# State-space outputs: states stored chunk-contiguous, all Toeplitz products first, then state products alternating over row halves and two PSUM banks

## The chip, the cores and the metric

The kernel runs on one core of a Trainium2 chip. The metric is the time of one execution on the device, in microseconds (us). The core has the matrix engine TensorE (PE; its weight loads are listed as PEld), VectorE (DVE), ScalarE (ACT), GpSimd (POOL) and SyncE (SP), which here mostly issues DMA transfers. Each engine works through a queue of its own, in order. PE multiplies a stationary operand, which is loaded first, with a moving one, and adds the result up in one of eight PSUM banks.

## What is computed

One layer of a decoder: normalisation, one input projection for two parallel parts, a sparse attention of eight heads and a state-space layer, then an output projection and a gated feed-forward network (FFN). The change concerns the state-space layer. For each of 32 groups of 16 channels it has 64 complex diagonal states:

```python
bu_re = jnp.einsum('blgi,gpi->blgp', uf, bb_re)
bu_im = jnp.einsum('blgi,gpi->blgp', uf, bb_im)
...
_, _, h_re, h_im = lax.associative_scan(complex_affine_combine, (ar, ai, bu_re, bu_im), axis=1)
y = (jnp.einsum('blgp,gip->blgi', h_re, prm['ssm_c_re'].astype(f32))
     - jnp.einsum('blgp,gip->blgi', h_im, prm['ssm_c_im'].astype(f32))
     + prm['ssm_d'].astype(f32) * uf)
```

The prompt has 1024 tokens, beside it there are 8 samples of 4 tokens. `y` goes through a gated linear unit (GLU) and, with the attention's output, into the output projection.

## The kernel before

The state-space layer is cut into 128 chunks of 8 tokens. A chunk's output is the sum of two parts: a Toeplitz product of the chunk's own inputs, and a product of the state before the chunk with C times powers of the eigenvalues. Groups go in pairs (two groups g of 64 states fill the 128 partitions), 16 pairs, four quarters Q of four pairs.

- `ssm_input` writes each chunk's contribution V (PE, line 1508) into the tile `H` (ssm_H; ACT, line 1511). `H` is laid out [128 states, 129 chunks, real/imaginary, 16 pairs].
- `ssm_scan` turns them into states: 128 steps of four DVE instructions of 32 elements each (lines 1526 to 1529), spread over the second phase, which is about the samples' attention and the first tiles of the prompt's.
- `ssm_powers` makes `Ct`, C times the powers, on POOL.
- `ssm_kernel(Q)`, letter K in the plan, makes the Toeplitz matrices: products `Kp` for g = 0 and 1 (PE, line 1576), four copies each, alternately on ACT and DVE (line 1579), an addition of the direct term `dd` on DVE (line 1584), and eight DMA loads on SP into `W[Q % 2]` (ssm_W, line 1586).
- `ssm_output(Q)`, letter Y, makes the outputs: for each g one PSUM bank `Y` with four pairs j side by side. For each j stand one Toeplitz product (line 1599, stationary operand the inputs ssm_UT, 128 rows) and two states' products (line 1601, stationary operand `self.H[P[g], 0:128, i, jj]`, 64 rows, one of real and imaginary part i). All are fp32 and each is two instructions on PE. ACT copies the bank out (line 1603). Then come the samples' outputs `Ys` in the same way (lines 1610, 1613, 1616), and DMAs to y_d and ys_d.

These pieces stand between the products of the prompt's attention (`phase_attend`, the third phase). Eight tiles of 128 prompt tokens are treated in the order 4, 0, 6, 1, 7, 2, 5, 3, each in four units (branch br, half hf): scores `as` for four heads (PE, lines 1195, 1196, 1199), maximum `asm` (DVE, line 1211), exponential `ap` (ACT, line 1212), then transposes (line 1269) and values `aso` (line 1273); `acs` (line 1248) and `aco` belong to the compressed branch. `PLAN` names what goes between the units, so for tile 0: nothing, nothing, `K0 K1 Y0`, `K2 Y1`; for tile 6: `K3 Y2`, `Y3 S`, `W G7`, `T4 G8 T5`. S are the last states, W the GLU's weights, G its tiles, T the second part of the modulation, P the output projection's weights.

The program's order is a wish: the framework's scheduler fixes each engine's own order at build time, by its own simulation, within the limits that buffers set. PSUM in this phase has a tag "s" of two tiles of two banks each, "t" with two banks, "o" and "f" with one each. Scores take "s". Within the planned pieces `ps_t` gives the one bank of "f" (`tags, self.tags = self.tags, "ff"`), so `Kp`, `Y` and `Ys` of the kernel before all go through that one bank, one after another.

Of the kernel before, what the change touches and what calls it, by code (L numbers as in the profile page):

```python
# [20 lines left out]
D = 1024  # L21
NT = 8          # tiles of 128 prompt tokens
NK = 8          # tiles of 128 input features
# [5 lines left out]
def shape_constants():  # L29
    """Constants that depend on shapes and positions alone, packed as [128, n] columns."""  # L30
# [27 lines left out]
    # sample rows are (batch in the half, token, group, head in the group)  # L58
# [31 lines left out]
class Kernel:  # L90
# [35 lines left out]
    def psum(self, name, **tags):  # L126
        self.pp = self.open(name, space=PS)
        self.pbufs = tags
        self.tags = "to"
        for t in tags:      # the banks go to the tags in this order  # L130
            self.pp.tile([128, 512 * (2 if t == "s" else 1)], F32, tag=t, name=f"{name}_{t}", bufs=tags[t])
# [23 lines left out]
    def load_constants(self, ea):  # L155
# [26 lines left out]
        nc.vector.tensor_scalar(self.gain_q, self.gain_q, 0.125, None, op0=ALU.mult)     # with the scores' scale  # L182
        # vectors over features, turned to feature-major: b_ada 48, norm_mix_g 8, norm_ffn_g 8, attn_out_g 4, ssm_out_g 4
# [12 lines left out]
    # ---- 1/sqrt(x * a + b), elementwise, on a small tile: a guess from the exponent, scaled by c, and three of Newton's  # L196
    # steps without their factor of -1/2, so that the scale turns c into -2 c^3, three times, and ends at one ----
    def rsqrt(self, x, a, b, name, eng=None, tag="", pool=None, bufs=3):
# [5 lines left out]
        # the guess: the bits of (magic - half of the bits) with c in its exponent and sign  # L204
        V.tensor_scalar(y.bitcast(I32), s.bitcast(I32), -0.5, float(0x5F3759DF) + math.log2(-c) * 2 ** 23 - 2 ** 31, op0=ALU.mult, op1=ALU.add)
        for _ in range(3):
            V.tensor_tensor(t, y, y, op=ALU.mult)
            V.tensor_tensor(t, t, s, op=ALU.mult)
            if eng:     # only the vector engine does both at once
# [22 lines left out]
    def ada_features(self, nb, ev, out):  # L232
        """out [128 feature, 4, 9] for the four 128-feature blocks, with the bias."""
# [8 lines left out]
    def ada_rows(self, nb, ev, pool, dst):  # L242
        """the nine rows, with the bias, to DRAM."""
# [34 lines left out]
    def phase_project(self):  # L278
        self.psum("psa", s=2, t=3, o=1)
        self.adaT = self.cst.tile([128, 4, 8, 9], F32, name="adaT")   # shift1, (1 + scale1) gain, and the FFN's  # L280
# [92 lines left out]
    def prep_c(self, pa):  # L373
        """silu of the nine conditions, feature-major; they come as rows (row, k-tile) of 128."""
# [26 lines left out]
    def gather(self, out, cache, b, j):  # L401
        """four positions of each of the 128 16-position chunks of a batch's paged rows: [128, 1024]."""
# [4 lines left out]
    def split(self, raw, hi, lo):  # L407
        """raw = hi + lo, each of twelve bits."""
        self.nc.scalar.copy(hi, raw)  # L409
        self.nc.vector.tensor_tensor(lo, raw, hi.bitcast(F32), op=ALU.subtract)  # L410

    def compress_weights(self, pa, pb):
# [4 lines left out]
        for i, s in enumerate("kv"):  # L417
# [16 lines left out]
            # the encodings' part of the hidden layer: products summed over the positions, then over the partitions  # L434
# [13 lines left out]
    def compress(self, b, cp):  # L448
        """the compressed keys and values of a paged batch (the ninth is the prompt), four positions of each chunk at a
        time; the products of one part follow the turning of the next, and the output's product comes later still."""  # L450
# [23 lines left out]
    def c_turn(self, b, j, cp):  # L474
        """four positions turned and split, two positions times 64 on the partitions: [(hi, lo)] of keys and values."""
# [27 lines left out]
    def c_product(self, b, j, X, cp):  # L503
        """their part of the hidden layer, for the blocks that begin and the blocks that end with the chunk."""
# [51 lines left out]
    def gelu2(self, out, x, t):  # L556
        """twice the tanh form of gelu: x (1 + tanh(sqrt(2 / pi) (x + 0.044715 x^3))); t is scratch."""
# [7 lines left out]
    def sigmoid2(self, out, z):  # L565
        """twice the sigmoid: 1 + tanh(z / 2)."""
# [31 lines left out]
    def sample_modulate(self, xn, out, iscale, ishift, p):  # L598
        """xn [32, 1024] normalised rows to feature-major modulated out [128, 8, 32]."""
# [10 lines left out]
    def sample_qkv(self, ea, sa):  # L610
# [20 lines left out]
        # gates, as rows (b, t, g, r) of three  # L631
# [7 lines left out]
        # queries, block-diagonal over the two groups  # L639
# [22 lines left out]
    def sample_attend(self, half, sb):  # L662
        """a half of the sample batches; rows (batch, token, group, head). The keys come in runs of 512 cached ones
        (the last run of a branch has the new ones behind it), each with its own maximum; the runs are weighed at the end. It goes in seven steps,
        the second half's between the products of the prompt's attention."""
# [7 lines left out]
        # compressed branch  # L673
# [15 lines left out]
        # importance of the 30 blocks that are not forced, the ranks, the mask of those not among the best 13  # L689
# [27 lines left out]
        # the new keys' scores, of both other branches  # L717
# [42 lines left out]
        # weights of the runs: exp(their maximum - the largest) gate / sum; M holds the maxima negated  # L760
# [1128 lines left out]
```

## Time and profile before

| | us |
|---|---|
| median of 3 runs | 1857.84 |
| lowest and highest | 1857.72 to 1870.4 |
| span of the profiled execution | 1867.2 |
| PE busy in it | 1779.7 (95%) |

The profile is of one execution by itself. Its page gives the span, 1867.2 us from the first to the last instruction, and no other time for that execution; it is 9.4 us above the median of the runs. Times of single instructions and of gaps come from this execution. "PEclk" is the granted clock of PE as a share of its full speed. The views give, beside the page, groups of instructions by line, single rows in order of time, sums over windows of time, and the chain of waits that ended last.

### The profile page before, as it was taken

The numbers are of one execution on the slowest core, as the hardware profiler recorded it, in microseconds if no ns is written. First come the engines' busy times: TensorE is split into PE (matmuls) and PEld (weight loads), VectorE is DVE, ScalarE is ACT, GpSimd is POOL, SyncE is SP. The second block draws the span as 40 slices with busy tenths as digits, with TensorE's granted clock in tenths as the row PEclk, the third lists the DMA queues.
The fourth block names the chain that finished last, engine by engine and source line by source line (L and its number), as shares of the span: only waits on it lengthen the run. The fifth ranks groups of instructions, "written<-read, shape, count | busy, mean of one in ns | idle before, by whom it ended". The sixth has DMA issues, their size and how long they took to land.

```text
span 1867.2 us, 29377 instructions
## 1 busy us (share of the span) xinstructions
PE 1779.7 (95%) x11546; PEld 1476.4 (79%) x11546; DVE 953.9 (51%) x2330; ACT 632.4 (34%) x1263; POOL 423.4 (23%) x817
## 2 busy tenths in 40 slices
PE   6898999899898999999989989999999999999997
PEld 3788998777655676565658889999999999999996
DVE  4867657667978433655755452332332332332346
ACT  4422146455555342565643341211211211211210
POOL 2334645232025310333112210100100100100140
PEclk9999999999899886999999999999999999999999
DMA  8333244544141111544225331201201201201113
GB/s 290 103 83 111 73 141 125 214 149 157 58 142 66 27 37 31 174 158 155 87 91 178 102 113 46 68 23 46 68 23 46 68 23 46 68 23 46 51 46 139
DMA packets 132700, 172.44 MB, mean 92 GB/s; under 512 B 17177, under 2 KB 92313, under 8 KB 132305
## 3 DMA queue, kind: packets, MB, share of 16 engines
q1 hardware_dynamic: 123024, 136.62, 23.0%
q0 software_dynamic: 9408, 33.89, 5.7%
q8 instruction: 91, 1.49, 0.3%
q14 instruction: 49, 0.39, 0.1%
q10 hardware_dynamic: 128, 0.04, 0.0%
HBM read 143.88 MB, written 25.46 MB: 91 GB/s over the span
## 4 chain that ended last, share of the span: by engine, by line
PE 83%; DVE 8%; DMA 4%; ACT 3%; issue 2%; POOL 0%; SPq 0%; another core or an unknown queue 0%; DVEq 0%; ACTq 0%; POOLq 0%
PE gu L1793 18%; PE dn L1836 13%; PE g L1793 5%; PE u L1793 4%; PE cp L516 4%; PE aso L1273 4%; PE Y L1601 2%; PE as L1195 2%; PE ss L823 1%; PE as L1196 1%; PE q0p L927 1%; PE ct L494 1%; PE q1p L927 1%; PE u1p L927 1%; PE kv0p L927 1%
## 5 line engine op out<-in xcount | busy, mean ns | idle before, releaser
L1793 PE MATMUL gu<-h2h,wh 128*128 128x352 f32 x704 | 227.9, 324 | 5.0 <-ACT h2h L860 5.0
L1793 PE MATMUL gu<-h2h,wl 128*128 128x352 f32 x704 | 227.4, 323 | 0.0
L1793 PE MATMUL gu<-h2l,wh 128*128 128x352 f32 x704 | 226.9, 322 | 0.0
L1842 DVE TENSOR_TENSOR acc<-acc,dn 128x512 f32<-128x512 f32 x144 | 98.8, 686 | 229.6 <-PE dn L1836 229.6
L1801 POOL TENSOR_TENSOR al<-fa,ah 128x352 fp32r<-128x352 f32 (+1 forms) x66 | 69.5, 1053 | 415.1 <-ACT ah L1800 408.8
L1796 ACT ACTIVATE fa<-gu 128x352 f32<-128x352 f32 x44 | 20.4, 465 | 412.5 <-PE gu L1793 412.5
L1836 PE MATMUL dn<-dh,ah 128*128 128x512 f32 x352 | 140.4, 399 | 5.2 <-DVE fin L1845 4.6
L1793 PEld LDWEIGHTS gu<-h2h,wh 128*128 128x128 f32 x704 | 132.6, 188 | 7.9 <-ACT h2h L860 5.3
L1836 PE MATMUL dn<-dl,ah 128*128 128x512 f32 x352 | 138.7, 394 | 0.0
L1836 PE MATMUL dn<-dh,al 128*128 128x512 f32 x352 | 138.3, 393 | 0.0
L1793 PEld LDWEIGHTS gu<-h2l,wh 128*128 128x128 f32 x704 | 133.0, 189 | 3.8
L1793 PEld LDWEIGHTS gu<-h2h,wl 128*128 128x128 f32 x704 | 132.9, 189 | 3.0
L409 ACT CAST wh<-wr 128x1024 fp32r<-128x1024 f32 x44 | 46.0, 1048 | 154.2 <-PE g L1793 77.0
L1799 DVE TENSOR_TENSOR fa<-fa,gu 128x352 f32<-128x352 f32 x44 | 22.9, 521 | 143.8 <-ACT fa L1796 143.8
L1195 PE MATMUL as<-kst,aqA 128*128 128x320 f32 (+4 forms) x192 | 79.7, 420 | 7.0 <-ACT ap L1212 2.9
L1836 PEld LDWEIGHTS dn<-dh,ah 128*128 128x128 f32 x352 | 66.1, 188 | 24.3 <-ACT wh L409 7.5
L410 DVE TENSOR_TENSOR wl<-wr,wh 128x1024 fp32r<-128x1024 f32 x44 | 58.8, 1338 | 49.8 <-ACT wh L409 49.8
L1836 PEld LDWEIGHTS dn<-dl,ah 128*128 128x128 f32 x352 | 66.1, 188 | 15.6
L1836 PEld LDWEIGHTS dn<-dh,al 128*128 128x128 f32 x352 | 66.3, 188 | 8.1
L1211 DVE TENSOR_REDUCE asm<-as 128x1 f32<-128x640 f32 (+3 forms) x64 | 58.7, 921 | 26.1 <-PE as L1199 25.5
L1196 PE MATMUL as<-kst,aqB 128*128 128x320 f32 (+4 forms) x192 | 67.4, 355 | 4.4 <-ACT aqB L1158 4.2
L1212 ACT ACTIVATE ap<-as,asm 128x640 f32<-128x640 f32 (+3 forms) x64 | 55.8, 874 | 27.4 <-DVE asm L1211 17.4
(2135 smaller groups left out, 4735.6 us busy)
## 6 DMA issues: line engine op xcount, KB each, us to landing
wada<-in_w_ada SPq DMA_DIRECT2D x24, 1024.0 KB
wr<-in_w_ffn_gate SPq DMA_DIRECT2D x22, 512.0 KB
wr<-in_w_ffn_up SPq DMA_DIRECT2D x22, 512.0 KB
wd<-in_w_ffn_down SPq DMA_DIRECT2D x22, 512.0 KB
bx<-in_x_prompt SPq DMA_DIRECT2D x8, 512.0 KB
s_raw<-in_cache_kv_win SPq DMA_DIRECT2D x8, 512.0 KB
wor<-in_w_out SPq DMA_DIRECT2D x16, 256.0 KB
ex<-x_d SPq DMA_DIRECT2D x8, 512.0 KB
```

What stands on the lines that cost most here:

```text
L410: self.nc.vector.tensor_tensor(lo, raw, hi.bitcast(F32), op=ALU.subtract)
L516: nc.tensor.matmul(P[:, 256 * ab:256 * ab + 256], w[:, 8 * ab + 2 * j + i, :], x[:, i, :], start=j == 0 and i == 0 and n == 0 and ab == 0, ...
L927: nc.tensor.matmul(p[:, t, :n], h[:, k, tok], ww[:, k % 4, :n], start=m == 0, stop=m == 23)
L1195: nc.tensor.matmul(Sv, qA[:, h, :], kk, start=True, stop=False)
L1196: nc.tensor.matmul(Sv, qB[:, h, :], kk, start=False, stop=not mt)
L1211: nc.vector.tensor_reduce(mx[:, :1], Sv, axis=ax, op=ALU.max, negate=True)
L1212: nc.scalar.activation(Pv, Sv, AF.Exp, bias=mx[:, :1], accum_out=l[:, h:h + 1])
L1273: nc.tensor.matmul(O[64 * g:64 * g + 64, 256 * hf:256 * hf + 256], V[:n, 64 * g:64 * g + 64], pT[:, 256 * g:256 * g + 256], start=first, s ...
L1793: nc.tensor.matmul(gu[i], w[:, k, :], h[:, k, 352 * n:352 * n + 352], start=m == 0, stop=m == 23)
L1801: nc.gpsimd.tensor_tensor(al[:, cols], a[:, :w], ah[:, cols].bitcast(F32), op=ALU.subtract)
L1836: nc.tensor.matmul(p, a[:, sl], w[:, c], start=m == 0, stop=m == 5)
L1842: nc.vector.tensor_tensor(o, o, p, op=ALU.add)
```

## The change

`H` is stored as [128 states, real/imaginary, 16 pairs, 129 chunks], so the 128 chunks of one pair lie next to each other: the stationary operand of a states' product is contiguous, while a step of the scan and the last state are read and written at a step of 129 elements, 516 bytes. `Y` becomes one tile of the tag "s" with a bank for each g. Its eight Toeplitz products come first; then the sixteen states' products in the order pair j, part i, group g, so that rows 0 to 63 with the first bank and rows 64 to 127 with the second alternate. ACT copies the bank of g = 0 out and DVE that of g = 1. `Ys` is changed likewise; its four copies take both groups at once. The count of matmuls stays. (The changed file also has no comments any more, which moves line numbers by a few.)

```diff
     def ssm_input(self, Q, sp, Bt):
...
-            nc.scalar.copy(self.H[:, 1:, :, jj], pv[:, :, :128].rearrange("p r c -> p c r"))
+            nc.scalar.copy(self.H[:, :, jj, 1:], pv[:, :, :128])
             nc.vector.tensor_copy(self.Hs[:, :, :, jj], pv[:, :, 128:])
...
     def ssm_scan(self, ss):
...
-            h = H[:, c]
-            hx = bass.AP(tensor=h.tensor, offset=h.offset + 16, ap=[h.ap[0], [-16, 2], [1, 16]])
+            h = H[:, :, :, c]
+            hx = bass.AP(tensor=h.tensor, offset=h.offset + 16 * 129, ap=[h.ap[0], [-16 * 129, 2], [129, 16]])
             V.tensor_tensor(t[0], LA[:, 0], h, op=ALU.mult)
             V.tensor_tensor(t[1], LA[:, 1], hx, op=ALU.mult)
             V.tensor_tensor(t[0], t[0], t[1], op=ALU.add)
-            V.tensor_tensor(H[:, c + 1], H[:, c + 1], t[0], op=ALU.add)
+            V.tensor_tensor(H[:, :, :, c + 1], H[:, :, :, c + 1], t[0], op=ALU.add)
...
-            nc.tensor.transpose(p[:16, :128], H[:, 128, i], self.ident)
+            nc.tensor.transpose(p[:16, :128], H[:, i, :, 128], self.ident)
...
     def ssm_output(self, Q):
...
+        Y = self.ps_s(f"Y{Q}")
         for g in G:
-            Y = self.ps_t(f"Y{Q}{g}")
             for j in range(4):
-                jj = 4 * Q + j
-                y = Y[:, 128 * j:128 * j + 128]
-                nc.tensor.matmul(y, self.UT[:, 2 * jj + g, :128], Wf[:, 2 * j + g], start=True, stop=False)
-                for i in range(2):
-                    nc.tensor.matmul(y, self.H[P[g], 0:128, i, jj], Ct[i][P[g], j, 1:9, :].rearrange("p t o -> p (t o)"),
-                                     start=False, stop=i == 1)
-            nc.scalar.copy(o[:, :, :, g, :].rearrange("c t j o -> c j t o"), Y.rearrange("c (j t o) -> c j t o", j=4, t=8))
+                nc.tensor.matmul(Y[:, g, 128 * j:128 * j + 128], self.UT[:, 8 * Q + 2 * j + g, :128], Wf[:, 2 * j + g],
+                                 start=j == 0, stop=False, skip_group_check=True)
+        for j in range(4):
+            for i in range(2):
+                for g in G:
+                    nc.tensor.matmul(Y[:, g, 128 * j:128 * j + 128], self.H[P[g], i, 4 * Q + j, 0:128],
+                                     Ct[i][P[g], j, 1:9, :].rearrange("p t o -> p (t o)"), start=False, stop=i == 1, skip_group_check=True)
+        for g in G:
+            (nc.vector.tensor_copy if g else nc.scalar.copy)(o[:, :, :, g, :].rearrange("c t j o -> c t j o"),
+                                                             Y[:, g].rearrange("c (j t o) -> c j t o", j=4, t=8))
...
+        Ys = self.ps_s(f"Ys{Q}")
         for g in G:
-            Ys = self.ps_t(f"Ys{Q}{g}")
             for j in range(4):
-                nc.tensor.matmul(Ys[32 * j:32 * j + 8, :64], self.UT[:, 8 * Q + 2 * j + g, 128:136], Wf[:, 2 * j + g, 64:], start=True, stop=False)
-            for i in range(2):
-                for j in range(4):
-                    nc.tensor.matmul(Ys[32 * j:32 * j + 8, :64], self.h0[P[g], i, :, 4 * Q + j],
-                                     Ct[i][P[g], j, 1:5, :].rearrange("p t o -> p (t o)"), start=False, stop=i == 1)
+                nc.tensor.matmul(Ys[32 * j:32 * j + 8, g, :64], self.UT[:, 8 * Q + 2 * j + g, 128:136], Wf[:, 2 * j + g, 64:],
+                                 start=True, stop=False, skip_group_check=True)
+        for i in range(2):
             for j in range(4):
-                nc.vector.tensor_copy(o[:, :, j, g], Ys[32 * j:32 * j + 8, :64].rearrange("c (t o) -> c t o", t=4))
+                for g in G:
+                    nc.tensor.matmul(Ys[32 * j:32 * j + 8, g, :64], self.h0[P[g], i, :, 4 * Q + j],
+                                     Ct[i][P[g], j, 1:5, :].rearrange("p t o -> p (t o)"), start=False, stop=i == 1, skip_group_check=True)
+        for j in range(4):
+            (nc.scalar.copy if j % 2 else nc.vector.tensor_copy)(
+                o[:, :, j].rearrange("c t g o -> c g t o"), Ys[32 * j:32 * j + 8, :, :64].rearrange("c g (t o) -> c g t o", t=4))
...
     def ssm_start(self, ss, si):
...
-        self.H = self.small(ss, [128, 129, 2, 16], "ssm_H")
+        self.H = self.small(ss, [128, 2, 16, 129], "ssm_H")
         self.Hs = self.small(ss, [128, 2, 8, 16], "ssm_Hs")
-        nc.vector.memset(self.H[:, 0], 0.0)
+        nc.vector.memset(self.H[:, :, :, 0], 0.0)
```

With the new tiles the scheduler also builds another order. PE's queue before, at the first piece of Y (quarter 0, g = 0): numbers behind names count buffers, Ct_7715 is the real part's and Ct_7716 the imaginary part's; a row is one matmul as the program writes it.

```order
L1269 MATMUL as601pt_8589<-ident,ap_8339 128x128
L1599 MATMUL Y_8067<-ssm_W_7711,ssm_UT_7709 128x128
L1601 MATMUL Y_8067<-Ct_7715,ssm_H 128x128
L1601 MATMUL Y_8067<-Ct_7716,ssm_H 128x128
L1599 MATMUL Y_8067<-ssm_W_7711,ssm_UT_7709 128x128
L1601 MATMUL Y_8067<-Ct_7715,ssm_H 128x128
L1601 MATMUL Y_8067<-Ct_7716,ssm_H 128x128
```

The two kinds of product change places after every one or two, and scores and values of the attention follow the piece. PE's queue after, from the last values of tile 6's first unit to Y1 (Kp_8041 is K1 for g = 1, Kp_8136 is K2 for g = 0, Y_8175 and ssm_W_7712 are quarter 1's):

```order
L1273 MATMUL aso_8335<-as606pT_8390,vst 64x256 x2
L1598 MATMUL Y_8067<-ssm_W_7711,ssm_UT_7709 128x128 x8
L1603 MATMUL Y_8067<-Ct_7715,ssm_H 128x128 x2
L1603 MATMUL Y_8067<-Ct_7716,ssm_H 128x128 x2
L1576 MATMUL Kp_8041<-Ct_7725,ssm_par 16x128 x4
L1576 MATMUL Kp_8041<-Ct_7726,ssm_par 16x128 x4
...
L1614 MATMUL Ys_8096<-ssm_W_7711,ssm_UT_7709 8x64 x8
L1619 MATMUL Ys_8096<-Ct_7715,ssm_par 8x64 x8
L1619 MATMUL Ys_8096<-Ct_7716,ssm_par 8x64 x8
L1576 MATMUL Kp_8136<-Ct_7735,ssm_par 16x128 x4
L1576 MATMUL Kp_8136<-Ct_7736,ssm_par 16x128 x4
L1598 MATMUL Y_8175<-ssm_W_7712,ssm_UT_7709 128x128 x8
```

The rows left out are the other twelve states' products of Y0. Between Y0 and Y1 no scores or values stand any more, and the second half of K1 is inside Y0. The scores of tile 6's second unit stood among K0's products before, one head of them here:

```order
L1195 MATMUL as_8337<-kst,aqA_7916 128x512
L1196 MATMUL as_8337<-kst,aqB_7917 128x512
L1195 MATMUL as_8337<-kst,aqA_7916 128x384
L1196 MATMUL as_8337<-kst,aqB_7917 128x384
L1199 LDWEIGHTS identb
L1199 MATMUL as_8337<-mk,identb 128x128
L1269 MATMUL as601pt_8358<-ident,ap_7940 128x128
```

After, all four heads of that unit stand behind Ys1 and the first Kp of K3:

```order
L1619 MATMUL Ys_8204<-Ct_7726,ssm_par 8x64 x8
L1576 MATMUL Kp_8400<-Ct_7745,ssm_par 16x128 x4
L1576 MATMUL Kp_8400<-Ct_7746,ssm_par 16x128 x4
L1195 MATMUL as_8295<-kst,aqA_7916 128x512
L1196 MATMUL as_8295<-kst,aqB_7917 128x512
L1195 MATMUL as_8295<-kst,aqA_7916 128x384
```

Later pieces follow: the GLU's tiles, the modulation's blocks and the output projection's weights stand earlier in the queues than before. The order of the scan's instructions on DVE is the same.

## Rows read from the trace of the kernel before

**Rows 1.** The page: span, busy time of PE, weight loads and the other engines.

```profile
span 1867.2 us, 29377 instructions
...
PE 1779.7 (95%) x11546; PEld 1476.4 (79%) x11546; DVE 953.9 (51%) x2330; ACT 632.4 (34%) x1263; POOL 423.4 (23%) x817
```

**Rows 2.** Windows (us, length, busy time by engine) at low and full clock.

```profile
core 0: us, PE busy (x) PEld busy (x) DVE busy (x) ACT busy (x) POOL busy (x), PEclk, DMA share, GB/s
...
619.00:626.00 7.00, 7.00 (x27) 4.97 (x29) 2.28 (x5) 1.47 (x3) 4.01 (x10) 0.51 0.11 19
...
639.50:660.00 20.50, 20.50 (x173) 13.99 (x171) 9.23 (x20) 10.34 (x24) 0.00 (x0) 1.00 0.10 16
...
704.30:724.80 20.50, 20.42 (x117) 13.74 (x117) 4.01 (x12) 2.93 (x5) 0.00 (x0) 0.50 0.09 27
```

**Rows 3.** Windows of the seven low stretches, tile Y alone: their sum.

```profile
sum 58.70, PE 22.73 PEld 17.42 ACT 4.16; mean PE 3.25 PEld 2.49 ACT 0.59
```

**Rows 4.** Windows of the eight pieces of Y, instructions of Y alone.

```profile
615.21:621.56 6.35, 6.35 (x24) 5.07 (x24) 0.00 (x0) 0.80 0.28 45
...
713.33:720.75 7.42, 7.42 (x24) 5.63 (x24) 0.00 (x0) 0.50 0.01 2
...
sum 51.43, PE 51.43 PEld 41.07 ACT 0.00; mean PE 6.43 PEld 5.13 ACT 0.00
```

**Rows 5.** Tile Y: weight loads, xcount: ns min/median/max, first and last start.

```profile
L1601 PEld LDWEIGHTS Y<-Ct,ssm_H x128: 287/310/313, 615.5 to 729.8; 64*128 64x128 f32 x128
L1599 PEld LDWEIGHTS Y<-ssm_W,ssm_UT x64: 186/189/338, 615.1 to 728.6; 128*128 128x128 f32 x64
```

**Rows 6.** Chain of waits, 570 to 905 us: start us, us, what.

```profile
611.46 1.73 PE acs L1248 x16
...
617.08 1.07 PE Y L1601 x4
...
618.57 1.17 PE Y L1601 x4
```

**Rows 7.** Timeline of PE, 338 us: start us, us, engine, line, operation, xcount.

```profile
338.23 1.15 PE L1508 MATMUL V<-ssm_UT,BTs 128*64 128x136 f32 x16
```

**Rows 8.** Timeline of PE, 624 to 642 us.

```profile
624.84 1.12 PE L1273 MATMUL aso<-as600pT,vst 128*64 128x256 f32 x4
...
625.75 0.65 PE L1273 MATMUL aso<-as601pT,vst 128*64 128x256 f32 x4
...
641.24 0.41 PE L1613 MATMUL Ys<-Ct,ssm_par 64*8 64x64 f32 x16
```

**Rows 9.** Timeline, 608 to 621 us, all engines.

```profile
608.07 0.58 SPq L1582 DMA_DIRECT2D dd<-in_ssm_d  x1
...
609.93 0.58 DVE L1583 TENSOR_TENSOR dd<-dd,ident 16x128 f32<-16x128 f32 x1 [0.42 <-DMA dd<-in_ssm_d]
...
610.51 0.63 PE L1576 MATMUL Kp<-Ct,ssm_par 64*16 64x128 f32 x16
...
613.76 0.29 DVE L1579 COPY K<-Kp 16x128 f32<-16x128 f32 x1 [0.33 <-ACT K L1579]
...
614.69 1.08 DVE L1584 TENSOR_TENSOR K<-K,dd 16x128 f32<-16x128 f32 x1
...
615.83 5.07 SPq L1586 DMA_DIRECT2D ssm_W<-K  x8
```

**Rows 10.** Timeline of PE, 589 us; bracketed: idle before, and what ended it.

```profile
589.67 0.49 PE L1195 MATMUL as<-kst,aqA 128*128 128x512 f32 x1 [1.87 <-ACT ap L1212]
```

**Rows 11.** DVE by line: scan, reductions, contiguous and stepped; busy us, mean ns.

```profile
L1526 DVE TENSOR_TENSOR scan<-ssm_LA,ssm_H 128x32 f32<-128x32 f32 x128 | 24.0, 188 | 4.7 <-DVE ssm_H L1529 1.4 <-issue 1.1
...
L1211 DVE TENSOR_REDUCE asm<-as 128x1 f32<-128x1024 f32 x8 | 9.8, 1223 | 2.1 <-PE as L1199 2.0
...
L438 DVE TENSOR_REDUCE perk<-w1rawk 128x128 f32<-128x1024 f32 x2 | 3.8, 1916 | 0.0
```

**Rows 12.** Windows of 60 us from 340 to 580 us, all engines: their sum.

```profile
sum 240.00, PE 220.98 PEld 163.37 DVE 183.41 ACT 128.03 POOL 49.79; mean PE 55.24 PEld 40.84 DVE 45.85 ACT 32.01 POOL 12.45
```

More of the change, by code (lines that the diff above doesn't have):

```diff
@@ L1593, in ssm_output @@
         o = sp.tile([128, 8, 4, 2, 16], F32, tag="q4", name=f"y{Q}", bufs=3)
+        Y = self.ps_s(f"Y{Q}")
         for g in G:
-            Y = self.ps_t(f"Y{Q}{g}")
             for j in range(4):
-                jj = 4 * Q + j
-                y = Y[:, 128 * j:128 * j + 128]
-                nc.tensor.matmul(y, self.UT[:, 2 * jj + g, :128], Wf[:, 2 * j + g], start=True, stop=False)
-                for i in range(2):
-                    nc.tensor.matmul(y, self.H[P[g], 0:128, i, jj], Ct[i][P[g], j, 1:9, :].rearrange("p t o -> p (t o)"),
-                                     start=False, stop=i == 1)
-            nc.scalar.copy(o[:, :, :, g, :].rearrange("c t j o -> c j t o"), Y.rearrange("c (j t o) -> c j t o", j=4, t=8))
+                nc.tensor.matmul(Y[:, g, 128 * j:128 * j + 128], self.UT[:, 8 * Q + 2 * j + g, :128], Wf[:, 2 * j + g],
[6 more added lines that the diff above has]
+        for g in G:
+            (nc.vector.tensor_copy if g else nc.scalar.copy)(o[:, :, :, g, :].rearrange("c t j o -> c j t o"),
+                                                             Y[:, g].rearrange("c (j t o) -> c j t o", j=4, t=8))
         nc.sync.dma_start(self.y_d.rearrange("(c t) f -> c t f", t=8)[:, :, 128 * Q:128 * Q + 128],
```

## The prediction, made before the result was known

> **What bounds the kernel now.** I read the page first. The span is 1867.2 us and TensorE (PE) is busy for 95% of it [rows 1], so a change pays if it shortens what PE does or waits for. The states' products run from 615 to 730 us, in the third phase. There the windows show PE without a gap, and in seven stretches the granted clock at 0.50 to 0.51 [rows 2], that is 1.2 GHz instead of 2.4. The seven last 58.70 us in all, of which instructions of the tile Y fill 22.73 [rows 3], so 36 us of those stretches are other work, held up by the clock. The windows cut at the eight pieces of Y (four quarters Q, two halves g) give 51.43 us for Y altogether, and 7.42 for the one piece that lies wholly in a low stretch [rows 4].
>
> Why a piece takes so long is seen in two views. In the tile's view a weight load of a states' product (ssm_H as the stationary operand, 64 rows, read at a step of 32 words) takes 310 ns, one of a Toeplitz product (128 rows, contiguous) 189 [rows 5]. In the chain of waits four instructions of states' products take 1.07 us, 0.268 each; the next four start 1.49 us later, so the pair of Toeplitz instructions between takes 0.42, or 0.21 each; a piece at full clock is 4 x 1.49 = 6.0 us. Sixteen instructions in a row with contiguous loads of the same width (acs) take 1.73 us, 0.108 each [rows 6]. At half clock a piece grows by a quarter only, from 6.0 to 7.42, so it is not the array's clock that sets it but the load, and the change back and forth between 128 and 64 rows.
>
> **The change, part by part.** The number of matmuls stays: per quarter 16 Toeplitz instructions and 32 of states.
>
> *Toeplitz products first.* They stand in a block with contiguous loads, as acs does: 16 x 0.108 = 1.7 us a quarter [rows 6]; 3.4 before.
>
> *States' products contiguous and alternating.* No row of before alternates between row halves with loads of this kind, so I bound the pace. From below: the products V, 16 instructions in 1.15 us or 0.072 each, whose loads are contiguous and 64 columns wide and whose halves of the output alternate [rows 7]. From above: the pace of now, 0.268. The contiguous load without any overlap of halves is acs, 0.108, and it is nearest: same 128 columns, a shorter stream in place of fewer rows. I take 0.11, so 32 x 0.11 = 3.5 us a quarter. For the changes between full and half height, now two or three a quarter instead of sixteen, I set 1.0 us. A quarter of Y is then 1.7 + 3.5 + 1.0 = 6.2, all four 25, between 18 (0.072, and half of the changes) and 45 (0.268). Against 51.4 that is **-26.4 us**, all of it on the path, since PE has no gap there.
>
> The rows show a strided 64-row load at 310 ns and a contiguous 128-row load at 189 [rows 5]. The Trainium skill, "TensorE: Matmul & The Clock Gate", LDWEIGHTS (loading the stationary operand), states that a load's time follows its column count and not its rows; by that the new layout brings nothing to these loads and the sum ends at rival 1. The trace does not agree, since loads of 128 columns differ by 1.6 times in it, so I go by the rows.
>
> *The clock.* Low stretches begin a few us into a piece of Y: the first at 619.0, with the piece begun at 615.21 [rows 2, 4]. From 639.5 to 660, with one piece in 20 us, the clock is full and PE just as busy [rows 2]. The same products at half clock take 1.12 us where they take 0.65 at full clock [rows 8]; of the 36 us of other work, 42% or **-15 us** come back if the stretches go with the slow pieces. Bounds: 0 and -18.
>
> *The wait for W1.* Y now takes two-bank tiles from the tag of the attention's scores, so the order on PE changes: the four scores of tile 6's second half, which ran among K0's products, come behind Y0, Ys0, Y1 and Ys1. Nothing is then left between Ys0 and Y1 on PE but one Kp. Y1 needs W[1], and the last Kp for it stands inside Y0. Its chain is read from the second quarter now [rows 9]: Kp 0.6, four copies one after the other at 0.3, 1.3 with their hand-overs, the add 1.1, eight loads issued on SP over 5.07 us, and about 1.9 us from an issue to its landing (dd, issued at 608.07, is used at 609.93). From the start of Kp to the landing of the last load, whose issue starts 4.4 us after the first, I get 0.6 + 1.3 + 1.1 + 4.4 + 1.9 + 0.4 for gaps = 9.7 us. PE has behind that Kp 24 instructions of Y0 (2.6 us), 48 of Ys0 (16 take 0.41 [rows 8], so 1.2) and the Kp of K2 (0.6), 4.4 us. So PE waits 5.3 us, everything behind Y1 with it: **+5.3** (2 to 8). Before, scores and values stood there, so the chain was covered; vector and scalar engines idle in the wait too. No row shows the clock behind such a wait; I allow one more low stretch as long as the first, 7 us [rows 2], half of it lost: **+3.5** (0 to 7). Y2 and Y3 have scores between them and their K steps: 0.
>
> *Scores behind the Y tiles.* With two tiles in the tag, the last two of the four scores wait for the exponentials of the first. Now such a wait is 1.87 us [rows 10]; one more of that size: **+2** (0 to 4).
>
> *The scan and the other users of ssm_H.* The 512 DVE instructions of the scan keep their order. Three of four now step by 516 bytes. A DVE reduction with a stepped read of 1024 elements takes 1916 ns, a contiguous one 1223, 0.7 ns an element more; with 32 elements that is 22 ns on 188 [rows 11]. 384 x 22 ns = 8.4 us more of DVE between 340 and 580 us, where it is busy for 183 of 240 us and PE for 221 [rows 12]. The 57 us in which DVE idles hide most; I put **+2** (-1 to +8) on the path, since the scan hands its result through DVE's single queue. If that cover were gone it would be 8.4. The copy of V into ssm_H writes runs of 128 instead of pairs of steps: off the path, 0.
>
> *Evacuations and what follows.* Y's copy for g = 1 moves to DVE, Ys needs 16 copies instead of 32; both engines are busy for half of the time there or less [rows 2]: 0. Gating, modulation and output-weight fills move earlier in the queue; their loads have to come earlier on SP too. No row prices this; I set **+2** (-2 to +5).
>
> **Sum:** -26.4 - 15 + 5.3 + 3.5 + 2 + 2 + 2 = -26.6 us, on the 1867.2 us of the profiled span. That execution is 9.4 us above the median of the runs, 1857.84; the places concerned lie in the middle, so I carry the difference over: **1831 us**, 1.4% less. A measurement of this kernel can tell about 1% from no change. Own range of the forecast: 1820 to 1841.
>
> **Rivals.**
> 1. *The pace does not change.* The two halves don't run side by side and a switch of halves costs what the stride cost; the queue does hold the products alternating, but that does nothing. For it: 64-row products are slow today, and no row shows a fast one with alternating halves. Against it: loads differ with the stride in [rows 5], and V's alternation is fast. Y is 45, -6.4; half of the clock's gain stays, -7.5; the wait shrinks to 1 since PE has more to do behind Kp (24 x 0.268 = 6.4 us instead of 2.6); +6 for scores, scan and the rest: -7, **1851 us**.
> 2. *The clock stays low.* The stretches belong to the phase, not to slow Y pieces. For it: the stretch from 704.3 ran on for 20.5 us, over other work as well. Against it: full clock from 639.5 to 660. Then 12 of the 15 us are missing: **1843 us**.
> 3. *Everything overlaps.* V's pace of 0.072, 18 us for Y (-33), -15 by the clock, a wait of 4 and no further low stretch, +4 for scores, scan and the rest: -40, **1818 us**.
> 4. *Slower: the scan.* Each element of a scan step now lies 516 bytes from the next. If an instruction doubles, 384 x 188 ns = 72 us more DVE meet 57 us of idle DVE, of which half is usable as the steps are serial: 44 us late, against the 27 won: +17, **1875 us**. It decides from 27 + 28 = 55 us, or 143 ns more per instruction. The stepped reduction, 22 ns for 32 elements, speaks against it. No row here has a 516-byte step. The Trainium skill, "SBUF — State Buffer", Specifications (TRN2), says that every step to a new 16-byte line costs a penalty; by that each element of the scan now pays it, which is this rival, and the states' loads stop paying it.
>
> **How the numbers follow.** Forecast 0.50, rival 1 0.17, rival 2 0.14, rival 3 0.12, rival 4 0.07. The range takes in the forecast, rivals 2 and 3 with some us to the low side for unknown terms, and the near side of rival 1: 1813 to 1850. Faster by over 1% (under 1839): nearly all of the forecast, rival 3, a small part of rival 2: 0.64. Within 1%: the rest of these and rival 1, 0.29. Slower by over 1%: rival 4, 0.07.
>
> **What would show it.** In the profile after: Y as four pieces of about 6 us, each of them 16 instructions at 0.11 and 32 near 0.11 us; loads of ssm_H near 190 ns; the clock at 1.0 through most of 605 to 735 us; PE idle for about 5 us ahead of Y1, ended by the load of ssm_W; the scan's instructions at 190 to 220 ns. I am wrong if states' products stay above 0.2 us, if the low stretches remain with Y short, or if DVE fills up between 340 and 580 us and the third phase begins later.

## The result, and the profile after

The changed kernel takes 1835.97 us (median, 1832.96 to 1847.22) against 1858.66 before: 0.9875 of the time before, 95% interval 0.9843 to 0.9907, 23 us less. The forecast was 1831, between 1813 and 1850. The profiled execution is the slowest of the five, 1847.22 us; like the profile of before, its span lies 9.4 us above the median of the runs, and times of single instructions below are from it.

The page of the changed kernel gives the span, the busy times and the granted clock in 40 slices (tenths of full speed):

```profile
span 1845.4 us, 29371 instructions
...
PE 1745.5 (95%) x11546; PEld 1454.5 (79%) x11546; DVE 957.5 (52%) x2310; ACT 631.6 (34%) x1267; POOL 425.4 (23%) x817
...
PEclk9899999999898899999999999999999999999999
```

PE is busy for 34 us less than in [rows 1], and the span is 22 us shorter: 12 us of the gain went into idle time of PE. The view of the tile Y, to be set beside [rows 5], with the waits ahead of its instructions (us, times):

```profile
L1603 PEld LDWEIGHTS Y<-Ct,ssm_H x128: 182/188/334, 608.3 to 657.7; 64*128 64x128 f32 x128
...
L1598 PEld LDWEIGHTS Y<-ssm_W,ssm_UT x64: 186/192/338, 606.3 to 655.7; 128*128 128x128 f32 x64
...
  DMA ssm_W<-K: 5.9, 1
```

The load of a states' product fell from 310 to 188 ns, the figure of a Toeplitz product. PE's timeline over Y0 and Y1 shows the rest:

```profile
606.32 2.05 PE L1598 MATMUL Y<-ssm_W,ssm_UT 128*128 128x128 f32 x16
608.30 0.71 PE L1603 MATMUL Y<-Ct,ssm_H 64*128 64x128 f32 x8
...
609.50 1.61 PE L1603 MATMUL Y<-Ct,ssm_H 64*128 64x128 f32 x24
611.04 0.41 PE L1614 MATMUL Ys<-ssm_W,ssm_UT 128*8 128x64 f32 x16
...
611.63 0.70 PE L1576 MATMUL Kp<-Ct,ssm_par 64*16 64x128 f32 x16
618.26 3.75 PE L1598 MATMUL Y<-ssm_W,ssm_UT 128*128 128x128 f32 x16 [5.92 <-DMA ssm_W<-K]
621.95 1.23 PE L1603 MATMUL Y<-Ct,ssm_H 64*128 64x128 f32 x8
...
624.08 2.93 PE L1603 MATMUL Y<-Ct,ssm_H 64*128 64x128 f32 x24
```

From 609.50 to 611.04, 24 states' instructions take 0.064 us each, where one took 0.268 [rows 6]; sixteen Toeplitz instructions (606.32 to 608.30) take 1.98 us, 0.124 each. Ahead of Y1 PE waits 5.92 us for W1, and Y1 then takes nearly twice the time. Windows around the wait show it (us, length, busy time of PE, PEld, DVE, ACT and POOL, granted clock, share and GB/s of the DMA engines).

```profile
605.00:612.00 7.00, 7.00 (x142) 5.51 (x144) 2.42 (x7) 2.09 (x6) 7.00 (x9) 1.00 0.01 4
612.00:618.30 6.30, 0.38 (x14) 0.12 (x4) 0.94 (x3) 0.53 (x3) 6.30 (x9) 0.65 0.31 49
618.30:625.20 6.90, 6.90 (x50) 5.95 (x52) 1.22 (x5) 1.01 (x4) 1.62 (x7) 0.50 0.39 118
```

The clock was full before the wait, fell while PE stood, and was at 1.2 GHz (0.50) in all of the 6.9 us behind it that the last window covers. The 24 states' instructions from 624.08 to 626.94 take 2.86 us, still at that pace, so the stretch lasted some 9 us.

The windows cut by stage show where the gain goes later. The cuts are the end of the scan, the first Y, the last Y, the last scores, and the first product of the FFN (gu). Of the kernel before:

```profile
core 0: us, PE busy (x), PEclk, DMA share, GB/s
578.90:615.20 36.30, 30.10 (x247) 1.00 0.27 87
615.20:729.90 114.70, 114.43 (x724) 0.77 0.12 30
729.90:942.00 212.10, 202.87 (x1344) 0.97 0.41 137
942.00:1043.60 101.60, 98.54 (x533) 0.99 0.40 126
sum 464.70, PE 445.93; mean PE 111.48
```

Of the changed kernel, the same cuts:

```profile
574.00:606.30 32.30, 26.21 (x180) 0.84 0.30 97
606.30:657.80 51.50, 43.37 (x537) 0.87 0.25 59
657.80:931.50 273.70, 259.05 (x1705) 0.98 0.36 121
931.50:1020.80 89.30, 79.33 (x429) 0.96 0.32 101
sum 446.80, PE 407.97; mean PE 101.99
```

PE's busy time fell by 38.0 us in this part, and its idle time rose from 18.8 to 38.8: 8 us between the first and the last Y, 5 in the stage behind it, 7 in the last. The rest of the difference of the two spans lies ahead of the third phase, at the end of the scan (578.9 and 574.0). Over all profiles of this study that point lies between 567 and 579 us with the old layout and between 568 and 584 with the new one. The scan's instructions have 215 ns as the middle value where it was 191 (before, then after):

```profile
L1526 DVE TENSOR_TENSOR scan<-ssm_LA,ssm_H x128: 140/191/246, 250.4 to 577.6; 128x32 f32<-128x32 f32 x128
...
L1526 DVE TENSOR_TENSOR scan<-ssm_LA,ssm_H x128: 163/215/289, 252.1 to 572.7; 128x32 f32<-128x32 f32 x128
```

### The profile page after: what moved, and what is told of

The parts are those of the page before. It is cut to its first block, busy times and chain, and to the rows that moved or that the text cites. A ratio compares the mean times of both kernels' runs of the same rounds, so it can differ in the third digit from the quotient of the medians.

```text
span 1845.4 us, 29371 instructions
## 1 busy us (share of the span) xinstructions
PE 1745.5 (95%) x11546; PEld 1454.5 (79%) x11546; DVE 957.5 (52%) x2310; ACT 631.6 (34%) x1267; POOL 425.4 (23%) x817
## 3 DMA queue, kind: packets, MB, share of 16 engines
q8 instruction: 91, 1.49, 0.3%
## 4 chain that ended last, share of the span: by engine, by line
PE 82%; DVE 8%; DMA 5%; ACT 3%; issue 2%; POOL 1%; SPq 0%; DVEq 0%; ACTq 0%; POOLq 0%
PE gu L1800 18%; PE dn L1843 13%; PE g L1800 5%; PE u L1800 4%; PE cp L516 4%; PE aso L1273 4%; PE as L1195 2%; PE ss L823 2%; PE as L1196 1%; PE q0p L927 1%; PE kv1p L927 1%; PE q1p L927 1%; PE ct L494 1%; PE u1p L927 1%; PE ada L226 1%
## 5 line engine op out<-in xcount | busy, mean ns | idle before, releaser
L1803 ACT ACTIVATE fa<-gu 128x352 f32<-128x352 f32 x44 | 20.4, 465 | 412.9 <-PE gu L1800 412.9
```

## The experiments

My theory was that the stepped load sets the pace of the states' products, and that the two-bank tiles cost time, since they are taken from the scores. The rivals: the pace comes from the change between 128 and 64 rows; the alternation alone gives the gain; the tiles cost nothing. All ratios below are to the kernel before on the same chip. There it took 1858.66 us beside the changed kernel, 1857.85 beside e1_layout, e2_order, e3_halves and e4_onebank, 1868.94 beside e6_ylate, e7_ft, e8_again and e9_stride, and 1868.70 beside e4_again, e12_spread and e13_spread.

| kernel | ratio | 95% interval |
|---|---|---|
| changed kernel | 0.9875 | 0.9843 to 0.9907 |
| the same once more (e8_again) | 0.9875 | 0.9851 to 0.9900 |
| layout alone (e1_layout) | 0.9828 | 0.9801 to 0.9855 |
| order and banks alone (e2_order) | 0.9883 | 0.9854 to 0.9913 |
| without alternation (e3_halves) | 0.9920 | 0.9893 to 0.9948 |
| one bank, Toeplitz first, contiguous (e4_onebank) | 0.9783 | 0.9759 to 0.9807 |
| the same once more (e4_again) | 0.9773 | 0.9742 to 0.9804 |
| one bank, Toeplitz first, stepped (e9_stride) | 0.9881 | 0.9856 to 0.9906 |
| changed kernel, Y a unit later (e6_ylate) | 0.9863 | 0.9840 to 0.9885 |
| second bank from the transposes (e7_ft) | 0.9946 | 0.9929 to 0.9964 |
| changed kernel, Y spread, half of the way (e12_spread) | 0.9799 | 0.9767 to 0.9831 |
| changed kernel, Y spread over more units (e13_spread) | 0.9838 | 0.9807 to 0.9870 |

**Layout alone.** The changed kernel's layout with the `ssm_output` of before:

```diff
-                    nc.tensor.matmul(y, self.H[P[g], 0:128, i, jj], Ct[i][P[g], j, 1:9, :].rearrange("p t o -> p (t o)"),
+                    nc.tensor.matmul(y, self.H[P[g], i, jj, 0:128], Ct[i][P[g], j, 1:9, :].rearrange("p t o -> p (t o)"),
```

> Only the layout of the states is changed; the products of Y stand as in the kernel before (one bank at a time, a Toeplitz product and two states' products in turn). My theory, that the stepped load sets the pace: the four instructions of states' products fall from 1.07 us to about 0.65 (the change of height stays), a pair j from 1.49 to about 1.07, Y from 51 to 34 us, part of the low clock goes: 1858 - 17 - 5 = about 1836 to 1842. Rival, that the pace comes from the change between 128 and 64 rows: a pair j stays at 1.4 to 1.5 us and the time within 5 us of before.

The loads of the states' products, PE's timeline at the first pairs j of Y, and the window from the first to the last Y:

```profile
L1601 PEld LDWEIGHTS Y<-Ct,ssm_H x128: 182/187/188, 608.2 to 691.3; 64*128 64x128 f32 x128
...
608.23 0.71 PE L1601 MATMUL Y<-Ct,ssm_H 64*128 64x128 f32 x4
608.86 0.49 PE L1599 MATMUL Y<-ssm_W,ssm_UT 128*128 128x128 f32 x2
...
609.92 0.49 PE L1599 MATMUL Y<-ssm_W,ssm_UT 128*128 128x128 f32 x2
...
607.90:691.40 83.50, 82.70 (x725) 1.00 0.17 41
```

From one Toeplitz pair to the next (608.86 to 609.92) it is 1.06 us instead of 1.49, and the four states' instructions take 0.63 (608.23 to 608.86) instead of 1.07. The time fell by 30 us (1827.69 against 1857.85), more than I expected and more than the 14 that the 32 pairs give at full clock (32 x 0.43). PE's order is that of before, and the clock between the first and the last Y is 1.00 where it was 0.77. So PE's other work became shorter too: in the four stages Y fell from 51.4 [rows 4] to 33.7 us of PE's time and all the rest from 394.5 to 379.7. The rival, the change of height, falls as the main cause. The layout alone, at 0.9828, is at least as fast as the whole change: the intervals overlap only at their ends.

**Order and banks alone.** The changed `ssm_output` with the layout of before; the order on every row of PE is that of the changed kernel:

```diff
-                    nc.tensor.matmul(Y[:, g, 128 * j:128 * j + 128], self.H[P[g], i, 4 * Q + j, 0:128],
+                    nc.tensor.matmul(Y[:, g, 128 * j:128 * j + 128], self.H[P[g], 0:128, i, 4 * Q + j],
```

> Only the order and the two banks are changed, the states are stored as before; the order on TensorE is that of the changed kernel, row for row. My theory: the stepped loads stay at 310 ns and the states' products at 0.16 to 0.22 us, a quarter of Y takes 2 + 32 x 0.19 = 8 us, the wait for W1 is shorter by the longer Y0 (about 3 us): 1845 to 1852. Rival, that the order alone gives the gain: states' products near 0.07 us as in the changed kernel and the same time, about 1836. The scan's instructions return to 188 ns in both; if the scan's cost were on the path, 2 to 8 us come back here.

```profile
L1603 PEld LDWEIGHTS Y<-Ct,ssm_H x128: 288/310/312, 598.5 to 650.7; 64*128 64x128 f32 x128
...
600.17 2.91 PE L1603 MATMUL Y<-Ct,ssm_H 64*128 64x128 f32 x24
603.01 0.41 PE L1614 MATMUL Ys<-ssm_W,ssm_UT 128*8 128x64 f32 x16
...
608.40 3.75 PE L1598 MATMUL Y<-ssm_W,ssm_UT 128*128 128x128 f32 x16 [4.09 <-DMA ssm_W<-K]
```

PE's timeline has 24 states' instructions in 2.84 us (600.17 to 603.01), 0.118 each, with loads that still take 310 ns each. So the loads overlap, and more than without alternation, where the pace is 0.23 (e9_stride, below). My figure of 0.16 to 0.22 was too high. Nor is the rival's 0.07 there, but its time is: 1836.04 us, where I had expected 1845 to 1852. The ratio is that of the changed kernel within the intervals. By the pace alone the slower products cost 128 x 0.054 = 7 us; the wait for W1 is 1.8 us shorter and the scan has the shorter instructions, which leaves some 5 us, less than the intervals resolve.

**No alternation.** In the changed kernel the groups come one after the other, the banks and the layout stay:

```diff
-        for j in range(4):
-            for i in range(2):
-                for g in G:
+        for g in G:
+            for j in range(4):
+                for i in range(2):
                     nc.tensor.matmul(Y[:, g, 128 * j:128 * j + 128], self.H[P[g], i, 4 * Q + j, 0:128],
```

> The changed kernel with the two groups one after the other, so that row halves and banks don't alternate. If alternation gives the pace beyond the layout: states' products at 0.11 us instead of 0.067, a quarter of Y 5.7 instead of 4.2, in all 6 us more, of which 1 is saved in the wait for W1: 1840 to 1842. Rival, the layout alone gives it: 0.067 stays, 1836.

```profile
637.16 2.60 PE L1603 MATMUL Y<-Ct,ssm_H 64*128 64x128 f32 x24
639.70 0.41 PE L1614 MATMUL Ys<-ssm_W,ssm_UT 128*8 128x64 f32 x16
...
sum 450.20, PE 414.88; mean PE 103.72
```

24 instructions take 2.54 us (637.16 to 639.70), 0.106 each, the pace of acs in [rows 6]. So contiguous loads give 0.106 and the alternation takes that to 0.064. Row halves and banks change together in it; no run tells one from the other. In time the alternation is worth some 0.45%, 8 us, if the ratios of different chips may be compared; the intervals of the two versions overlap at their ends. The sum of the four stages, the last line, is used below.

**One bank for each group.** Contiguous states and Toeplitz products first, but each group in the one bank of tag f, as before:

```diff
         for g in G:
             Y = self.ps_t(f"Y{Q}{g}")
             for j in range(4):
+                nc.tensor.matmul(Y[:, 128 * j:128 * j + 128], self.UT[:, 8 * Q + 2 * j + g, :128], Wf[:, 2 * j + g],
+                                 start=j == 0, stop=False, skip_group_check=True)
+            for j in range(4):
+                for i in range(2):
+                    nc.tensor.matmul(Y[:, 128 * j:128 * j + 128], self.H[P[g], i, 4 * Q + j, 0:128],
...
```

> Contiguous states and Toeplitz products first, but one bank for each group, as in the kernel before, no alternation; TensorE's order between the pieces is then that of before, with scores and values between K1 and Y1. If the wait for W1 and the later order cost what I read (5.9 us, a low stretch of 3 to 4, some 8 of idle time in the gating and mixing), this gives Y at about 26 us, no wait for ssm_W, and 1825 to 1832, faster than the changed kernel in spite of slower products. Rival, that the two-bank tiles pay and their wait is filled elsewhere: 1838 to 1845.

PE's timeline of a piece:

```profile
607.25 1.06 PE L1597 MATMUL Y<-ssm_W,ssm_UT 128*128 128x128 f32 x8
608.24 2.05 PE L1601 MATMUL Y<-Ct,ssm_H 64*128 64x128 f32 x16
610.22 0.41 PE L1195 MATMUL as<-kst,aqA 128*128 128x320 f32 x1
```

And its window from the first to the last Y, with the sum of all four stages:

```profile
607.30:681.50 74.20, 73.41 (x725) 1.00 0.19 46
...
sum 421.20, PE 401.37; mean PE 100.34
```

This is the fastest version: 40 us under before on its chip (1818.09 us), and 0.9773 once more on another:

> The one-bank version once more, beside the two others on the same chip: 0.976 to 0.981 of before.

A piece takes 2.97 us (607.25 to 610.22) with the states' instructions at 0.124, nearly twice the 0.064 of the changed kernel. PE idles for 19.8 us in the four stages, as before (18.8), and the clock is full throughout Y. The version without alternation, which has the same loads and a like pace (0.106), has 0.9920 against 0.9783 here, 25 us more, and PE idles for 35.3 us in its four stages (450.20 less 414.88). The two differ in the tiles, and with them in the order on PE and in the engines that copy the banks out. Together that costs 25 us; the rival, that it is filled elsewhere, falls.

**One bank, stepped.** The same with the states stored as before:

```diff
-                    nc.tensor.matmul(Y[:, 128 * j:128 * j + 128], self.H[P[g], i, 4 * Q + j, 0:128],
+                    nc.tensor.matmul(Y[:, 128 * j:128 * j + 128], self.H[P[g], 0:128, i, 4 * Q + j],
```

> The one-bank version (Toeplitz first, order of before) with the states stored as before. This completes the square of layout and Toeplitz-first in the same order of pieces. My theory, that the stepped load sets the pace without alternation: states' products at 0.22 us, a piece 1.0 + 16 x 0.22 + 0.3 = 4.8 us against 2.97, Y 38 us, part of the low clock back: 1836 to 1848. Rival, that it was the change of height and not the step: a piece near 3.2 us and 1818 to 1822.

```profile
613.31 1.06 PE L1597 MATMUL Y<-ssm_W,ssm_UT 128*128 128x128 f32 x8
614.30 3.77 PE L1601 MATMUL Y<-Ct,ssm_H 64*128 64x128 f32 x16
```

Sixteen states' instructions take 3.7 us (614.30 to the next product at 618.00), 0.23 each against 0.124: without alternation the step costs a factor of 1.9. In time, with PE's order of before: layout alone 0.9828, Toeplitz first alone 0.9881, both 0.9783.

**Where the tiles' cost lies.** First only the plan of the changed kernel was moved, so that scores cover the wait for W1:

```diff
-0: ('', '', 'K0 K1 Y0', 'K2 Y1'), 6: ('K3 Y2', 'Y3 S', 'W G7', 'T4 G8 T5')
+0: ('', '', 'K0 K1', 'Y0 K2'), 6: ('Y1 K3', 'Y2 Y3 S', 'W G7', 'T4 G8 T5')
```

> The changed kernel with only the plan moved: Y0 comes with K2, Y1 with K3 and Y2 with Y3, each a unit of the attention later, so that on TensorE the four scores of tile 6's second unit stand between Ys0 and Y1. If the wait for W1 and the low clock behind it are the cost of the two-bank tiles: no wait on ssm_W, no low stretch near 620 us, 6 + 4 us less than the changed kernel, 1826 to 1830. Rival, that the cost lies in the later order (gating, mixing), which this leaves as it is: 1834 to 1838, with the wait gone and the idle time elsewhere.

The wait for ssm_W fell from 6.0 us to two of 1.6 in all, the clock is 1.00 in the two stages around Y. Yet the ratio is 0.9863, within the intervals of the changed kernel on the same chip, which was run beside it:

> The changed kernel as it is, once more beside these three on the same chip: the same 1830 to 1840, with the wait for ssm_W of 4 to 6 us ahead of Y1 and a low stretch behind it.

```profile
622.99 3.75 PE L1598 MATMUL Y<-ssm_W,ssm_UT 128*128 128x128 f32 x16 [6.01 <-DMA ssm_W<-K]
626.67 0.72 PE L1603 MATMUL Y<-Ct,ssm_H 64*128 64x128 f32 x8
```

It had the wait, 6.01 us, and a clock of 0.93 from the first to the last Y. Only the Toeplitz products behind the wait run at half pace here (3.68 us, to 626.67). The stages of the version with the later Y show PE idle for 17.8 us behind the last Y (14.5 in e8_again) and 8.5 in the last stage:

```profile
657.20:935.00 277.80, 260.04 (x1694) 0.98 0.35 116
935.00:1021.30 86.30, 77.82 (x435) 1.00 0.36 116
```

So the wait was removed and most of its gain given back; the rival is nearer. The last Y still ended at 657 us. In the trace of the changed kernel gating and modulation follow soon behind the last Y and end in tile 7, at 817 us, while before they lasted until 904 us, in tile 5. For tile 2 attention alone then remains on PE, and beside it ACT and DVE make the output weights (829.6 to 856.2 us). The next step moved the Y apart, with the same products:

```diff
-0: ('', '', 'K0 K1 Y0', 'K2 Y1'), 6: ('K3 Y2', 'Y3 S', 'W G7', 'T4 G8 T5'), 1: ('', '', '', '')
+0: ('', '', 'K0 K1', 'Y0 K2'), 6: ('Y1', 'K3', 'Y2', ''), 1: ('Y3 S', 'W G7', 'T4 G8 T5', '')
```

> Half of the way: the last Y is at the end of tile 6, the fills end in tile 2. By my theory the time lies between the changed kernel (0.9875) and the version with all Y apart, 0.980 to 0.985; by the rival no better than 0.986.

```profile
sum 426.20, PE 398.43; mean PE 99.61
```

It gives 0.9799, below the interval of the changed kernel, 14 us less; its PE idles for 27.8 us in the four stages instead of 38.8, and no wait for ssm_W is left ahead of Y. With its two-bank tiles it lies within the intervals of the one-bank version. Going further, with each piece from Y1 on one unit of the attention later,

```diff
+0: ('', '', 'K0 K1', 'Y0'), 6: ('K2', 'Y1', 'K3', 'Y2'), 1: ('', 'Y3 S', 'W G7', 'T4 G8 T5')
```

> The changed kernel's two-bank, alternating products, with only the plan moved: the four Y stand one unit of the attention or more apart, the last in tile 1, as they did before; the gating and the modulation, which wait for the last Y, then end near tile 5 as in the kernel before. My theory, that 15 to 20 us of the changed kernel's loss against the one-bank version come from this (Y done early, fills used up in tile 7, nothing left for TensorE in tiles 2, 5 and 3 while the output weights are made): 0.975 to 0.981 of before, equal to the one-bank version or better. Rival, that the score tiles themselves are too scarce with Y in them: a wait at each Y for the exponentials, 0.984 to 0.989.

```profile
sum 437.40, PE 405.68; mean PE 101.42
```

gave 0.9838, with 31.7 us of idle time, 14.0 of it between the last Y and the last scores. That is not the 0.975 to 0.981 of my theory but close to the rival's range. Its interval overlaps with that of e12_spread and with that of the changed kernel, so it can be told from neither. What is shown is that one plan with Y apart takes 14 us less than the changed kernel; that further apart is better is not shown, and what decides between the two plans was not settled.

**The second bank from the transposes.** Contiguous, and written to alternate, with one bank of f and one of t:

```diff
-        Y = self.ps_s(f"Y{Q}")
+        Y = [self.ps("ft"[g], f"Y{Q}{g}") for g in G]
```

> Contiguous states and alternating row halves over two banks, but the second bank is one of the two that the transposes use (the first the one of before), so no score tile is taken; the samples' outputs as before. If the alternation is worth what the row-half experiment shows (states' products 0.064 instead of 0.106 to 0.124 us) and the score tiles are the cost: 6 us less of Y than the one-bank version, 1812 to 1816. Rival, that taking a bank from the transposes shifts the order as much as the score tiles did: 1825 to 1845, with a wait on ssm_W or on the transposes' bank.

```profile
603.31 0.91 PE L1576 MATMUL Kp<-Ct,ssm_par 64*16 64x128 f32 x16 [1.91 <-DVE K L1579]
...
612.25 2.07 PE L1597 MATMUL Y<-ssm_W,ssm_UT 128*128 128x128 f32 x8 [3.26 <-DMA ssm_W<-K]
614.26 2.93 PE L1602 MATMUL Y<-Ct,ssm_H 64*128 64x128 f32 x12
617.12 2.07 PE L1597 MATMUL Y<-ssm_W,ssm_UT 128*128 128x128 f32 x8
```

The slowest of the changed versions, 0.9946, slower even than the rival's range. The rows show that it is not the kernel that I meant to run. The order that was built has eight Toeplitz instructions, twelve states' instructions and only then the other eight Toeplitz: the first twelve belong to one group, and the two groups come mostly one after the other. In the later quarters eight and sixteen follow each other at 0.124 us for a states' instruction at full clock. So there is no alternation in it to set against the place of a bank. K0 to Y1 stand nearly in one row on PE, which waits for the copies of K and for ssm_W; the clock is 0.78 and 0.82 in the stage ahead of the first Y and in that up to the last. That the new bank shifts the order, the rival's claim, holds.

## Why the prediction was right, step by step

- *States' products* (-26.4 us): direction and cause right, the size a little too small, -31. Y fills 20.4 us, not 25, though Y1 is at half clock: the pace is 0.064, below the end of 0.072 that I took from V. A quarter at full clock is 16 x 0.124 + 32 x 0.064 = 4.0 us, not 6.2; the 1.0 us that I set for changes of height is not to be seen in it. The layout brings a load from 310 to 188 ns and the pace without alternation to 0.106 (e3_halves), which is the 0.11 that I had put; the alternation, which I counted with nothing, gives the rest. That the new layout was needed I had not questioned: under alternation the stepped loads reach 0.118 (e2_order), and the time can't be told from the changed kernel's. Nor had I asked what the layout does alone, which took no more time than the whole change (e1_layout).
- *The clock* (-15, and 3.5 back): the long low stretches are gone with the slow pieces, in the one-bank version and with the layout alone entirely (1.00 through Y against 0.77). The low stretch behind the wait came, some 9 us where I allowed 7, and took Y1 with it. In the profiled execution a second one lay ahead of the first Y (0.84 in that stage, 0.94 in the repeat). So PE's work outside Y fell in the four stages by 7 us there (394.5 to 387.6) and by 14 in the repeat, where the sum has 11.5; the size of this term changes from execution to execution. Rival 2, that the clock belongs to the phase, is refuted by the two versions with 1.00.
- *The wait for W1* (+5.3): 5.92 us, and 6.01 in the repeat; *scores behind Y* (+2): 1.19 and 0.96.
- *The scan* (+2): 24 ns more per instruction where I had 22. That 22 came so near is in part luck: the two reductions that it was taken from also differ in the memory that they read (one the scores in PSUM, one a tile in SBUF) and in how many results they write. On the path the term is neither shown nor excluded. In single executions the scan ended at 567 us with the old layout and at 568 to 571 with the new on one chip, at 577 and at 581 to 584 on a second, and on the chip of the result 5 us earlier with the new. Rival 4, the slower outcome, needed 143 ns more.
- *What follows* (+2, with an end of +5) is the term that was mis-sized. PE's idle time rose by 5.4 us between the last Y and the last scores and by 6.9 from there to the FFN, 12 in all. I had seen that gating and weights move to earlier places and had counted it as nearly nothing. The plan of e12_spread shows that the wait for W1, its low stretch and part of this idle time, 14 us together, can be had back without a change to any product. Which of the moved instructions costs most is not shown.

Added up for the two profiled executions: -31 for Y, -7 for the clock, +6 for the wait for W1, +2 for the scores, +12 for what follows, and -4 ahead of the third phase and behind it, -22 in all where the sum has -26.6. The larger gain on Y and the larger loss behind it have opposite signs, so 1831 lies close to 1836. The main mechanism was right; that the total came so close is luck, since single terms are off by 4 to 10 us.

The Trainium skill's rule in "TensorE: Matmul & The Clock Gate", LDWEIGHTS (loading the stationary operand), does not hold for these stepped loads, since the same 128 columns went from 310 to 188 ns with the layout alone (e1_layout). What the Trainium skill says of steps to a new line in "SBUF — State Buffer", Specifications (TRN2), agrees in direction on both sides: 122 ns less for 128 elements of a weight load, 24 ns more for 32 elements of a scan step.

## What to carry to other kernels

A faster inner block is worth what the schedule around it leaves: here the tile class that the block takes its PSUM from, with the order that came with it, weighed 25 us, and the alternation that needed that class some 8. The one-bank version is 17 us faster than the changed kernel, and another plan with the same two-bank tiles won back 14 of them, so most of this lay in the order. Before moving a block to another class of buffers, look who rotates in it and what that moves past the block; try the block in the buffers it had first. And where a faster block ends early, see what filler work it sets free too soon for the stages that will need it.

## What the runs showed of the hardware

- Weight loads overlap, and more so when row halves and banks alternate: with loads of 310 ns the pace is 0.118 us an instruction against 0.23, with loads of 188 ns it is 0.064 against 0.106. Halves and banks were not changed apart.
- A contiguous weight load followed the clock of PE, a stepped one did not: Y's contiguous loads go from 188 ns to 334 in the low stretch of the changed kernel, while stepped ones stay between 287 and 313 before, with full and low stretches among them [rows 5]. So at half clock 24 contiguous alternating instructions take 2.86 us instead of 1.54, where a piece with stepped loads grew by a quarter only [rows 4, 6]. Whether the loads or the products set the pace of the contiguous ones was not separated.
- A wait of 5.9 us of PE was followed by some 9 us at 1.2 GHz, though the work behind it was dense. Behind 6.0 us in the repeat only the next 3.7 us were slow. The other pieces of Y of the changed kernel, behind a wait of 1 us or none, ran at full clock.
